# Attention with negated, pre-scaled scores, the sink as a 129th score column, and one copy of the whole product with the values

## Chip, core and metric

One Trainium2 chip, one NeuronCore. The metric is device time in microseconds (us), the median of several runs. The engines are PE (matrix products; PEld is its weight load), DVE (vector), ACT (scalar functions), POOL and SP (which issues the DMAs here). They run side by side and wait for each other by semaphores. Each one works through its own queue in order.

## The reference, cut to what matters

The program is one step of a two-layer decoder on 512 prompt rows and 8 sample rows. Layer 0 is a recurrent mixer, which the change leaves alone. Layer 1 is attention in a sliding window of 128 keys with 32 query heads in 4 groups of 8, and a learned "sink" score per head, which takes part in the softmax and has no value row:

```
ATTN_SCALE = HEAD_DIM ** -0.5        # 64 ** -0.5
def sink_softmax(s, sinks):
    sink = ...                        # one score per head, broadcast to every query
    pr = jax.nn.softmax(jnp.concatenate([s, sink], axis=-1), axis=-1)
    return pr[..., :-1]
def one_block(args):                  # 128 queries against 128 or 256 keys
    mask = in_band & ((cidx >= WINDOW) | (n > 0))
    s = jnp.einsum('bqhgd,bkhd->bhgqk', qn, kn) * ATTN_SCALE
    s = jnp.where(mask, s, -jnp.inf)
    pr = sink_softmax(s, sinks)
    return jnp.einsum('bhgqk,bkhd->bqhgd', pr, vn)
```

Each layer ends in `mix @ w_out`, a norm, and a gated embedding. The activations stand transposed in the kernel: features on partitions, rows (520 = 512 + 8) along the free axis.

## The kernel before

**Products in three parts.** An fp32 product is made of three faster ones: weights and activations are split into a high and a low half. ACT casts the high half (`wh` of the weights `wr`), DVE or POOL subtracts it for the low half (`wl`), and PE adds `wh` x high, `wl` x high and `wh` x low in a PSUM pair `pj`. These projection matmuls (128x260) are most of PE's work. Their operands `xs` are the split activations of the layer's input, `og` the split outputs of the attention, which the products with `w_out_b` read.

**The attention.** Layer 1 runs eight units `u` of four query heads. A unit has four projection tiles (two of queries, two of gates `z`). `query` applies the rotation to a tile `tmp` and splits each head's 64 rows into high and low, stacked on 128 partitions of a tile `g`. Then `block(u, st, n, osb)` runs for each of the four blocks `n` of 128 queries. It makes the scores of four heads in two PSUM banks `ph` (`xr` holds the keys); ACT copies them into the score tile `W` [128, 4, 128], and DVE's copy_predicated takes the masked part: the previous block's keys, or `neg` in the first block. DVE then finds the maximum `nm` (tile `an`), joins it with the sink (`sinkb`), forms the sink's exponent `es` (tile `ae`) and negates the maximum. ACT takes four exponentials with the scale 1/8, whose sums go to `den` (tile `ad`), and one of the sink. DVE adds that, takes the reciprocal and multiplies `W`. PE transposes `W` (`ident` on the left), the result is split into high and low (two tiles `g`), masked copies of these are made with `tmask`, and PE multiplies them with the values `V`. The two halves of the 128 result rows (high and low value columns) are added: ACT copies a half of the rows to `both` (tile `m`), and DVE adds the other half, into `osb` (tile `ao`). After the fourth block, `osb` is gated and split into the unit's `og`.

`W` lies in the buffers of the tags b2 (3) and b3 (2), which other stages share. `sample_b` serves the 8 sample rows of four units at a time, in one short sequence of its own (`qs`, `bm`, `bd`, `tmp`, `bo`).

**What sets the order.** The code does not issue instructions directly. `Plan.enter` records each with its reads and writes, and `Plan.issue` then sets the order of every engine's queue by a list schedule with costs written into the program. It places an instruction where it would start earliest by these costs. An instruction that may run on DVE or POOL (`nc.either`) is put on one of them there. All of PE's matmuls, projections and attention alike, stand in one queue in that order, so that a matmul that is not ready holds all behind it. Because every instruction is issued at line 162, the profile names that line throughout, and the groups are told apart by their tiles.

Of the kernel before, what the change touches and what calls it, by code (L numbers as in the profile page):

```python
# [18 lines left out]
P = 128  # L19
D_MODEL = 1024  # L20
KC = D_MODEL // P
SEQ = 512
# [6 lines left out]
HD = 64  # L29
EPS = 1e-6  # L30
SCALE = HD ** -0.5
NEG = -1.0e30
SWAP = list(range(8, 16)) + list(range(0, 8)) + list(range(16, 32))

PRE0, PRE1, POST0, POST1, KVG, ONORM, LB0, LB1 = 0, 8, 16, 24, 32, 40, 56, 72
# [322 lines left out]
class Step:  # L358
# [53 lines left out]
    def more_consts(self):  # L412
        nc, cp, i = self.nc, self.cp, self.i
        self.ident = cp.tile([P, P], F32, name="ident")
        nc.sync.dma_start(self.ident, i["ident"])
        self.pairmask = cp.tile([P, 64], F32, name="pairmask")
        nc.sync.dma_start(self.pairmask, i["pairmask"])
        self.ones_r = cp.tile([P, P], F32R, name="ones_r")
        nc.scalar.copy(self.ones_r, self.ones.to_broadcast([P, P]))
        self.lmask = self.plan.tile(self.sp, [P, 6, 64], I32, "lmask", "m", 1)  # L420
        nc.sync.dma_start(self.lmask.rearrange("p a b -> p (a b)"), i["lmask"])
        self.neg = cp.tile([P, 1], F32, name="neg")
        nc.vector.memset(self.neg, NEG)
        self.pmask = cp.tile([P, P], I32, name="pmask")
        nc.sync.dma_start(self.pmask, i["pmask"])
        self.tmask = cp.tile([P, 2, P], F32, name="tmask")
        nc.sync.dma_start(self.tmask.rearrange("p a b -> p (a b)"), i["tmask"])
        self.sinkb = cp.tile([P, 32], F32, name="sinkb")
        nc.sync.dma_start(self.sinkb, i["sinkb"])
        self.sinks = cp.tile([P, KVH // 2], F32, name="sinks")  # L430
        nc.sync.dma_start(self.sinks, i["sinks"])

# [131 lines left out]

    def rsqrt_small(self, ps, rows, cols, n, tag):
        nc = self.nc
        ms = self.small(tag + "m", [P, 8])
        nc.vector.tensor_scalar(ms[:rows, :cols], ps, 1.0 / n, EPS, op0=ALU.mult, op1=ALU.add)
        r = self.small(tag + "r", [P, 8])
        nc.gpsimd.tensor_tensor(r[:rows, :cols], ms[:rows, :cols], self.mhalf[:rows, :cols], op=ALU.pow)  # L570
        return r

# [518 lines left out]
    def unit_proj(self, u, xs, st, done):  # L1091

        nc = self.nc
        kvh = u // 2
        rows = slice((kvh % 2) * HD, (kvh % 2 + 1) * HD)
        st["Q"], st["z"], st["og"] = [], [], []

        def query(c):
            def evac(ps):
                q = self.tmp_()  # L1100
                self.rope(ps, self.C, self.S, q)
                for a in range(2):
                    s = self.g_(F32R)
                    me = slice(a * HD, (a + 1) * HD)
                    other = slice((1 - a) * HD, (2 - a) * HD)
                    nc.scalar.copy(s[me, :SEQ], q[me, :SEQ])
                    nc.vector.tensor_tensor(
                        s[other, :SEQ], q[me, :SEQ], s[me, :SEQ].bitcast(F32), op=ALU.subtract
                    )
# [43 lines left out]
    def block(self, u, st, n, osb):  # L1153


        nc = self.nc
        kvh = u // 2
        keys = P if n == 0 else 2 * P
        k0 = 0 if n == 0 else (n - 1) * P
        W = self.small("b3", [P, 4, P], 2) if n % 3 else self.small("b2", [P, 4, P], 3)  # L1160
        for a in range(2):
            ps = self.bank().rearrange("p (a k) -> p a k", a=2)
            for b in range(2):
                q = st["Q"][2 * a + b][:, n * P : (n + 1) * P]
                for K, s0, s1 in ((self.Kh, True, False), (self.Kl, False, True)):
                    nc.tensor.matmul(ps[:, b, :keys], q, K[kvh][:, k0 : k0 + keys], start=s0, stop=s1)
            w = W[:, 2 * a : 2 * a + 2]
            if n == 0:
                nc.scalar.copy(w, ps[:, :, :P])
                nc.vector.copy_predicated(  # L1170
                    w,
                    self.pmask.unsqueeze(1).to_broadcast([P, 2, P]),
                    self.neg.unsqueeze(1).to_broadcast([P, 2, P]),
                )
            else:
                nc.scalar.copy(w, ps[:, :, P:])
                nc.vector.copy_predicated(w, self.pmask.unsqueeze(1).to_broadcast([P, 2, P]), ps[:, :, :P])
        nm = self.small("an", [P, 4])
        nc.vector.tensor_reduce(nm, W, AX.X, ALU.max)
        sk = self.sinkb[:, 4 * u : 4 * u + 4]  # L1180
        nc.vector.scalar_tensor_tensor(nm, nm, SCALE, sk, op0=ALU.mult, op1=ALU.max)
        es = self.small("ae", [P, 4])
        nc.vector.tensor_tensor(es, sk, nm, op=ALU.subtract)
        nc.vector.tensor_scalar(nm, nm, -1.0, None, op0=ALU.mult)
        den = self.small("ad", [P, 4])
        for j in range(4):
            nc.scalar.activation(
                W[:, j], W[:, j], AF.Exp, bias=nm[:, j : j + 1], scale=SCALE, accum_out=den[:, j : j + 1]
            )
        nc.scalar.activation(es, es, AF.Exp)  # L1190
        nc.vector.tensor_tensor(den, den, es, op=ALU.add)
        nc.vector.reciprocal(den, den)
        nc.either.tensor_tensor(W, W, den.unsqueeze(2).to_broadcast([P, 4, P]), op=ALU.mult)
        pt = self.bank()
        for pos, j in enumerate((0, 2, 1, 3)):
            nc.tensor.transpose(pt[:, pos * P : (pos + 1) * P], W[:, j], self.ident)
        hi, lo = (self.g_(F32R, SEQ) for x in range(2))
# [3 lines left out]
        if n:  # L1201
            for x in (hi, lo):
# [5 lines left out]
                    op=ALU.mult,  # L1208
                )
                parts.append((2 * n - 1 if n < 3 else 4, y))  # L1210
        po = self.bank()
        for x, (vn, pp) in enumerate(parts):
            V = self.V[vn][:, kvh]
            nc.tensor.matmul(po, V, pp, start=x == 0, stop=x == len(parts) - 1)
        both = self.small("m", [P, 512], 1)
        for a in range(2):
            me = slice(a * HD, (a + 1) * HD)
            other = slice((1 - a) * HD, (2 - a) * HD)
            t = both[:, a * 256 : (a + 1) * 256]
            nc.scalar.copy(t[me], po[other, a * 256 : (a + 1) * 256])  # L1220
            nc.vector.tensor_tensor(
                osb[me, :, n * P : (n + 1) * P],
                po[me, a * 256 : (a + 1) * 256].rearrange("p (c t) -> p c t", c=2),
                t[me].rearrange("p (c t) -> p c t", c=2),
                op=ALU.add,
            )
        if n < NCH - 1:
            return
        for c, (hi, lo) in enumerate(self.og_b(u, st)):
            w = osb[:, c]  # L1230
# [396 lines left out]
```

## Time and profile before

| what | value |
|---|---|
| median of 3 runs | 1131.54 us (1131.02 to 1131.56) |
| profiled execution, its own time | 1133.34 us |
| its span, first to last instruction | 1131.5 us |
| PE / DVE / ACT / POOL busy | 1106.6 / 966.1 / 749.7 / 121.8 us |
| mean granted TensorE clock | 0.995 |
| DMA | 137.56 MB, mean 122 GB/s |

The span runs from the first layer (to about 600 us) over its gates and the keys and values to the attention units with their output products (about 660 to 1060) and the last gates. A row of a group of instructions reads: engine, operation, out<-in, shapes, count, then busy us and mean ns of one, then the engine's idle time before them and what ended it. A row of waits reads: engine and tile that waited, what released it, total us, number of waits, the longest. A row of stretches reads: from:to, length, then busy us and (xcount) of PE, PEld, DVE, ACT and POOL, then the granted clock, the DMA share and GB/s. A row of the timeline reads: start, duration, engine, operation, and in brackets the idle time before it and its releaser.

### The profile page before, as it was taken

To read this page: it belongs to the slowest core of one execution; us is meant where nothing else is said; L and a number is where in the kernel's file an instruction comes from. 1 tells how busy PE (TensorE), PEld (TensorE's weight loads), DVE (VectorE), ACT (ScalarE), POOL (GpSimd) and SP (SyncE) were. 2 spreads that over 40 slices of the span, in tenths; PEclk is the share of its full clock that TensorE was granted. 3 is DMA by queue.
4 is the path that set the end of the run, shared out by engine and by line. 5 is a ranking of instruction groups with operands and counts; after the bars stand their busy time and mean duration, and the time that the engine had idled before them with its cause. 6 is when DMAs were issued, how large, how long until landed. Compare 5 with 4: busy or idle time off the path is not lost.

```text
span 1131.5 us, 23984 instructions
## 1 busy us (share of the span) xinstructions
PE 1106.6 (98%) x8999; PEld 1088.3 (96%) x8999; DVE 966.1 (85%) x2218; ACT 749.7 (66%) x1990; POOL 121.8 (11%) x188
## 2 busy tenths in 40 slices
PE   8999999999999999999999999999989999999998
PEld 7999999999999999999999999999989999999997
DVE  6998888758888588888879989999988998998983
ACT  7878777657775477777736657767666764764551
POOL 0121121112211122111100000110100000000000
PEclk9999999999999999999999999999989999999999
DMA  8433524334432343434445442212212222312532
GB/s 292 150 135 115 187 99 170 110 136 152 139 126 97 118 165 134 143 125 138 141 151 204 127 152 91 77 57 86 84 39 75 76 75 75 107 49 73 205 104 86
DMA packets 53821, 137.56 MB, mean 122 GB/s; under 512 B 10948, under 2 KB 18124, under 8 KB 53704
## 3 DMA queue, kind: packets, MB, share of 16 engines
q1 hardware_dynamic: 53704, 136.02, 35.7%
q8 instruction: 71, 1.16, 0.4%
q14 instruction: 46, 0.38, 0.1%
HBM read 119.22 MB, written 16.77 MB: 120 GB/s over the span
## 4 chain that ended last, share of the span: by engine, by line
PE 70%; DVE 20%; ACT 5%; issue 3%; DMA 1%; POOLq 0%; SPq 0%; POOL 0%; DVEq 0%; ACTq 0%
PE pj L162 56%; PE ph L162 14%; DVE g L162 4%; DVE tmp L162 3%; DVE wl L162 3%; DVE b L162 2%; ACT b L162 1%; DVE ao L162 1%; DVE an L162 1%; DVE xr L162 1%; DMA wr<-in_w_pg 1%; DVE x L162 1%; ACT tmp L162 1%; ACT g L162 1%; ACT wh L162 1%
## 5 line engine op out<-in xcount | busy, mean ns | idle before, releaser
L162 PE MATMUL pj<-xs,wh 128*128 128x260 f32 x3328 | 571.2, 285 | 0.8 <-DVE x L162 0.3
L162 PEld LDWEIGHTS pj<-xs,wh 128*128 128x128 f32 x3328 | 468.9, 189 | 4.1 <-ACT xs L162 1.2
L162 PE MATMUL pj<-xs,wl 128*128 128x260 f32 x1664 | 346.6, 285 | 0.0
L162 PEld LDWEIGHTS pj<-xs,wl 128*128 128x128 f32 x1664 | 260.7, 189 | 0.8
L162 ACT CAST wh<-wr 128x512 fp32r<-128x512 f32 x288 | 176.3, 618 | 97.9 <-PE pj L162 87.0
L162 DVE TENSOR_TENSOR wl<-wr,wh 128x512 fp32r<-128x512 f32 x273 | 188.1, 692 | 31.3 <-ACT wh L162 29.9
L162 PE MATMUL pj<-og,wh 128*128 128x260 f32 x1056 | 187.3, 287 | 2.5 <-ACT g L162 1.4
L162 PEld LDWEIGHTS pj<-og,wh 128*128 128x128 f32 x1056 | 152.9, 190 | 4.7 <-DVE x L162 1.8
L162 PE MATMUL pj<-og,wl 128*128 128x260 f32 x512 | 108.0, 286 | 0.0
L162 ACT ACTIVATE tmp<-pj 128x520 f32<-128x520 f32 (+1 forms) x93 | 48.0, 528 | 55.0 <-PE pj L162 54.5
L162 PEld LDWEIGHTS pj<-og,wl 128*128 128x128 f32 x512 | 81.3, 190 | 0.6
L162 ACT ACTIVATE sb<-sb,nv 128x128 f32<-128x128 f32 x128 | 68.4, 564 | 0.2
L162 ACT ACTIVATE sb<-sb,g 128x128 f32<-128x128 f32 x128 | 64.3, 561 | 4.5 <-DVE sb L162 4.2
L162 DVE COPY_PREDICATED xr<-lmask,ph 128x128 f32<-128x128 int32 x192 | 55.2, 323 | 5.3 <-PE ph L162 4.1
L162 PE MATMUL pj<-xs,b 128*128 128x260 f32 x384 | 52.2, 285 | 2.8 <-ACT b L162 2.0
L162 DVE TENSOR_TENSOR x<-x,pj 128x520 f32<-128x520 f32 (+1 forms) x80 | 46.0, 582 | 10.6 <-PE pj L162 9.9
L162 ACT ACTIVATE b<-b,an 128x128 f32<-128x128 f32 x128 | 50.4, 396 | 2.9 <-DVE an L162 2.7
L162 PEld LDWEIGHTS pj<-xs,b 128*128 128x128 f32 x384 | 48.2, 188 | 3.9 <-ACT b L162 2.4
L162 PE MATMUL ph<-g,b 128*128 128x512 f32 x112 | 46.1, 424 | 3.5 <-DVE g L162 2.6
L162 PE MATMUL ph<-b,xr 128*128 128x256 f32 (+1 forms) x288 | 47.5, 281 | 0.0
L162 DVE TENSOR_TENSOR xr<-xr,b 128x256 f32<-128x256 f32 x96 | 41.2, 430 | 4.8 <-PE ph L162 3.0
L162 ACT COPY xr<-ph 32x64 f32<-32x64 f32 (+2 forms) x128 | 39.7, 313 | 8.5 <-PE ph L162 6.1
(208 smaller groups left out, 1861.6 us busy)
## 6 DMA issues: line engine op xcount, KB each, us to landing
wr<-in_w_in_a SPq DMA_DIRECT2D x64, 512.0 KB, 3.6
sb<-sd SPq DMA_DIRECT2D x32, 512.0 KB, 4.7
wr<-in_w_in_b SPq DMA_DIRECT2D x32, 512.0 KB, 3.5
sb<-in_state SPq DMA_DIRECT2D x16, 512.0 KB, 5.0
out_st_s<-sb SPq DMA_DIRECT2D x16, 512.0 KB, 2.9
wr<-in_w_out_a SPq DMA_DIRECT2D x16, 512.0 KB, 3.8
wr<-in_w_pg SPq DMA_DIRECT2D x16, 512.0 KB, 4.3
wr<-in_w_out_b SPq DMA_DIRECT2D x16, 512.0 KB, 3.5
```

The costliest lines, as they stand in the source:

```text
L162: op = Op(len(self.ops), self.level, on, [lambda c=c: c(*a, **k) for c in calls], [self.price(e, name, ins, a, k) for e in on], on[0] == " ...
```

## The change

- The query split writes -1/8 times the queries, so the scores leave PE negated and scaled. The masked value becomes +1e30 (`far`), the maximum a minimum, and the exponentials take scale -1 with the minimum as bias.
- `W` gets a 129th column per head, filled by ACT with the negated sink ahead of the scores. Minimum and sums of the exponentials cover it, so that the join, the sink's exponent, its exponential, its addition and the negation of the maximum go away. `sinkb` is negated once at the start.
- ACT copies all 128 rows of the product with the values at once; DVE's two additions take one half from PSUM and the other from that copy.
- Two small tiles of the sample rows' norm in layer 0 (tag "nn") have one buffer in place of two.

```
# query
-  nc.scalar.copy(s[me, :SEQ], q[me, :SEQ])
-  nc.vector.tensor_tensor(s[other, :SEQ], q[me, :SEQ], s[me, :SEQ].bitcast(F32), op=ALU.subtract)
+  nc.scalar.activation(s[me, :SEQ], q[me, :SEQ], AF.Copy, scale=-SCALE)
+  nc.vector.scalar_tensor_tensor(
+      s[other, :SEQ], q[me, :SEQ], -SCALE, s[me, :SEQ].bitcast(F32), op0=ALU.mult, op1=ALU.subtract)
# block
-  W = self.small("b3", [P, 4, P], 2) if n % 3 else self.small("b2", [P, 4, P], 3)
+  W = self.small("b3", [P, 4, P + 1], 2) if n % 3 else self.small("b2", [P, 4, P + 1], 3)
+  nc.scalar.copy(W[:, :, P], self.sinkb[:, 4 * u : 4 * u + 4])
...
-  nc.vector.tensor_reduce(nm, W, AX.X, ALU.max)
-  sk = self.sinkb[:, 4 * u : 4 * u + 4]
-  nc.vector.scalar_tensor_tensor(nm, nm, SCALE, sk, op0=ALU.mult, op1=ALU.max)
-  es = self.small("ae", [P, 4])
-  nc.vector.tensor_tensor(es, sk, nm, op=ALU.subtract)
-  nc.vector.tensor_scalar(nm, nm, -1.0, None, op0=ALU.mult)
+  nc.vector.tensor_reduce(nm, W, AX.X, ALU.min)
   den = self.small("ad", [P, 4])
   for j in range(4):
       nc.scalar.activation(
-          W[:, j], W[:, j], AF.Exp, bias=nm[:, j : j + 1], scale=SCALE, accum_out=den[:, j : j + 1])
-  nc.scalar.activation(es, es, AF.Exp)
-  nc.vector.tensor_tensor(den, den, es, op=ALU.add)
+          W[:, j], W[:, j], AF.Exp, bias=nm[:, j : j + 1], scale=-1.0, accum_out=den[:, j : j + 1])
   nc.vector.reciprocal(den, den)
...
   both = self.small("m", [P, 512], 1)
+  nc.scalar.copy(both, po)
   for a in range(2):
-      t = both[:, a * 256 : (a + 1) * 256]
-      nc.scalar.copy(t[me], po[other, a * 256 : (a + 1) * 256])
-      nc.vector.tensor_tensor(osb[me, :, n * P : (n + 1) * P], po[me, ...], t[me], op=ALU.add)
+      nc.vector.tensor_tensor(osb[me, :, n * P : (n + 1) * P], of(po, other), of(both, me), op=ALU.add)
# more_consts
+  nc.vector.tensor_scalar(self.sinkb, self.sinkb, -1.0, None, op0=ALU.mult)
```

Since the costs are recorded from the code, the planner sets another order for the whole attention stage; the first layer's order stays. In the rows below, the numbers behind a tile's name are its own; before and after count differently.

First place, on PE, where unit 3's projections end and the products with `w_out_b` of units 0 and 1 run. Before: behind the scores of unit 3's last block (`ph_2051`) come the transposes of unit 2's last block (`b2_1957`), then its products with the values (`ph_1968`), with the sample rows' product (`ph_2005`) between.

```order
L162 MATMUL ph_2051_2147<-xr_1678_1774,g_1992_2088 128x256
L162 MATMUL ph_2051_2147<-xr_1682_1778,g_1992_2088 128x256
L162 MATMUL ph_2051_2147<-xr_1678_1774,g_1993_2089 128x256
L162 MATMUL ph_2051_2147<-xr_1682_1778,g_1993_2089 128x256
L162 MATMUL ph_1963_2059<-ident_109,b2_1957_2053 128x128 x4
L162 MATMUL ph_1968_2064<-g_1964_2060,b4_1652_1748 128x512
L162 MATMUL ph_2005_2101<-tmp_2004_2100,b3_1995_2091 128x16 x8
L162 MATMUL ph_1968_2064<-g_1965_2061,b4_1652_1748 128x512
L162 MATMUL ph_1968_2064<-g_1966_2062,b2_1653_1749 128x512
L162 MATMUL ph_1968_2064<-g_1967_2063,b2_1653_1749 128x512
L162 MATMUL pj_2091_2187<-og_1786_1882,wh_2017_2113 128x260
```

After, at the same place (the end of the projection `pj_2004`, the sample rows' product `ph_1993`): the transposes are those of unit 3's first block (`b2_2013`), and 19 projection matmuls follow before its product with the values, five rows of which are shown.

```order
L162 MATMUL ph_2037_2133<-xr_1682_1778,g_1981_2077 128x256
L162 MATMUL pj_2004_2100<-xs_1621_1717,wh_1996_2092 128x260 x2
L162 MATMUL ph_1993_2089<-tmp_1992_2088,b3_1983_2079 128x16 x8
L162 MATMUL ph_2018_2114<-ident_109,b2_2013_2109 128x128 x4
L162 MATMUL pj_2071_2167<-og_1782_1878,wh_1999_2095 128x260
L162 MATMUL pj_2071_2167<-og_1782_1878,wl_2000_2096 128x260
L162 MATMUL pj_2071_2167<-og_1783_1879,wh_1999_2095 128x260
L162 MATMUL pj_2071_2167<-og_1784_1880,wh_1999_2095 128x260
L162 MATMUL pj_2071_2167<-og_1784_1880,wl_2000_2096 128x260
```

Unit 2's last block (`b2_1946` after) has its transposes 51 rows further up now, inside that projection:

```order
L162 MATMUL pj_2004_2100<-xs_1606_1702,wl_1977_2073 128x260 x2
L162 MATMUL pj_2004_2100<-xs_1607_1703,wh_1976_2072 128x260
L162 MATMUL ph_1984_2080<-qs_1697_1793,b4_1982_2078 128x16 x8
L162 MATMUL ph_1951_2047<-ident_109,b2_1946_2042 128x128 x4
L162 MATMUL pj_2004_2100<-xs_1607_1703,wh_1976_2072 128x260
```

The block has moved from the end of the projections into them.

Second place, on DVE, the same block (unit 2, `n` = 3), from its reduction on. Before: up to the negated maximum, for which ACT's exponentials wait.

```order
L162 TENSOR_REDUCE an_1960_2056<-b2_1957_2053 128x4
L162 TENSOR_SCALAR tmp_2001_2097<-tmp_2001_2097,bd_2002_2098 128x128
L162 SCALAR_TENSOR_TENSOR an_1960_2056<-an_1960_2056,sinkb_116 128x4
L162 TENSOR_TENSOR g_1952_2048<-ph_1950_2046,g_1951_2047 128x512
L162 TENSOR_TENSOR g_1953_2049<-g_1951_2047,tmask_115 128x512
L162 TENSOR_TENSOR g_1954_2050<-g_1952_2048,tmask_115 128x512
L162 TENSOR_TENSOR ae_1961_2057<-sinkb_116,an_1960_2056 128x4
L162 COPY_PREDICATED b2_2025_2121<-pmask_114,neg_113 128x256
L162 TENSOR_SCALAR an_1960_2056<-an_1960_2056 128x4
```

After: from the reduction, for which the exponentials wait, to the reciprocal of the sums.

```order
L162 TENSOR_REDUCE an_1949_2045<-b2_1946_2042 128x4
L162 SCALAR_TENSOR_TENSOR g_1970_2066<-tmp_1968_2064,g_1970_2066 64x512
L162 SCALAR_TENSOR_TENSOR g_1971_2067<-tmp_1968_2064,g_1971_2067 64x512
L162 TENSOR_TENSOR tmp_1978_2074<-pj_1972_2068,ropeC_1630 128x520
L162 STREAM_SHUFFLE tmp_1979_2075<-pj_1972_2068 128x520
L162 TENSOR_TENSOR g_1941_2037<-ph_1939_2035,g_1940_2036 128x512
L162 TENSOR_TENSOR tmp_1979_2075<-tmp_1979_2075,ropeS_1631 128x520
L162 TENSOR_TENSOR wl_1997_2093<-wr_1975_2071,wh_1996_2092 128x512
L162 TENSOR_TENSOR tmp_1978_2074<-tmp_1978_2074,tmp_1979_2075 128x520
L162 TENSOR_TENSOR g_1943_2039<-g_1941_2037,tmask_115 128x512
L162 RECIPROCAL ad_1950_2046<-ad_1950_2046 128x4
```

The three small instructions between the reduction and the exponentials are gone, and so is the addition ahead of the reciprocal.

Third place, on ACT: after, the sink's column of a score tile (`b2_2047`) stands behind the cast (`CAST g_1952`) of the transposes of the tile that had the buffer before (`b2_1946`).

```order
L162 CAST g_1952_2048<-ph_1951_2047 128x512
L162 COPY b2_2047_2143<-sinkb_116 128x4
L162 COPY b2_2013_2109<-ph_2015_2111 128x2x128
L162 COPY b3_2023_2119<-ph_2025_2121 128x2x128
L162 ACTIVATE be_1988_2084<-be_1988_2084 128x1
```

Before, ACT's first instruction on a score tile was the copy of its first scores; now it is the sink's column.

More of the change, by code (lines that the diff above doesn't have):

```diff
@@ L31 @@
 SCALE = HD ** -0.5
-NEG = -1.0e30
+FAR = 1.0e30
 SWAP = list(range(8, 16)) + list(range(0, 8)) + list(range(16, 32))
@@ L421, in more_consts @@
         nc.sync.dma_start(self.lmask.rearrange("p a b -> p (a b)"), i["lmask"])
-        self.neg = cp.tile([P, 1], F32, name="neg")
-        nc.vector.memset(self.neg, NEG)
+        self.far = cp.tile([P, 1], F32, name="far")
+        nc.vector.memset(self.far, FAR)
         self.pmask = cp.tile([P, P], I32, name="pmask")
@@ L566, in rsqrt_small @@
         nc = self.nc
-        ms = self.small(tag + "m", [P, 8])
+        bufs = 1 if tag == "nn" else 2
+        ms = self.small(tag + "m", [P, 8], bufs)
         nc.vector.tensor_scalar(ms[:rows, :cols], ps, 1.0 / n, EPS, op0=ALU.mult, op1=ALU.add)
-        r = self.small(tag + "r", [P, 8])
+        r = self.small(tag + "r", [P, 8], bufs)
         nc.gpsimd.tensor_tensor(r[:rows, :cols], ms[:rows, :cols], self.mhalf[:rows, :cols], op=ALU.pow)
@@ L1105, in evac @@
                     other = slice((1 - a) * HD, (2 - a) * HD)
-                    nc.scalar.copy(s[me, :SEQ], q[me, :SEQ])
-                    nc.vector.tensor_tensor(
-                        s[other, :SEQ], q[me, :SEQ], s[me, :SEQ].bitcast(F32), op=ALU.subtract
+                    nc.scalar.activation(s[me, :SEQ], q[me, :SEQ], AF.Copy, scale=-SCALE)
+                    nc.vector.scalar_tensor_tensor(
+                        s[other, :SEQ], q[me, :SEQ], -SCALE, s[me, :SEQ].bitcast(F32), op0=ALU.mult, op1=ALU.subtract
                     )
@@ L1166, in block @@
                     nc.tensor.matmul(ps[:, b, :keys], q, K[kvh][:, k0 : k0 + keys], start=s0, stop=s1)
-            w = W[:, 2 * a : 2 * a + 2]
+            w = W[:, 2 * a : 2 * a + 2, :P]
             if n == 0:
@@ L1172, in block @@
                     self.pmask.unsqueeze(1).to_broadcast([P, 2, P]),
-                    self.neg.unsqueeze(1).to_broadcast([P, 2, P]),
+                    self.far.unsqueeze(1).to_broadcast([P, 2, P]),
                 )
@@ L1187, in block @@
             nc.scalar.activation(
-                W[:, j], W[:, j], AF.Exp, bias=nm[:, j : j + 1], scale=SCALE, accum_out=den[:, j : j + 1]
+                W[:, j], W[:, j], AF.Exp, bias=nm[:, j : j + 1], scale=-1.0, accum_out=den[:, j : j + 1]
             )
-        nc.scalar.activation(es, es, AF.Exp)
-        nc.vector.tensor_tensor(den, den, es, op=ALU.add)
         nc.vector.reciprocal(den, den)
+        W = W[:, :, :P]
         nc.either.tensor_tensor(W, W, den.unsqueeze(2).to_broadcast([P, 4, P]), op=ALU.mult)
@@ L1218, in block @@
             other = slice((1 - a) * HD, (2 - a) * HD)
-            t = both[:, a * 256 : (a + 1) * 256]
-            nc.scalar.copy(t[me], po[other, a * 256 : (a + 1) * 256])
[L1221 to L1226, printed above, removed]
+            of = lambda x, rows: x[rows, a * 256 : (a + 1) * 256].rearrange("p (c t) -> p c t", c=2)
+            nc.vector.tensor_tensor(osb[me, :, n * P : (n + 1) * P], of(po, other), of(both, me), op=ALU.add)
         if n < NCH - 1:
```

## The prediction

> **What bounds the kernel now.** I read the page's first part, then busy time by stage, then what TensorE waits for in the stage that the change touches.
>
> ```profile
> PE 1106.6 (98%) x8999; PEld 1088.3 (96%) x8999; DVE 966.1 (85%) x2218; ACT 749.7 (66%) x1990; POOL 121.8 (11%) x188
> 660.00:1060.00 400.00, 391.69 (x3095) 380.50 (x3094) 371.44 (x863) 257.98 (x781) 20.46 (x16) 0.99 0.26 85
> ```
>
> The second row is the attention stage: PE (391.69 of 400) and DVE (371.44) are both nearly full, ACT is not. A busy PE may be slow, so the pace matters:
>
> ```profile
> 948.38 14.11 PE pj L162 x118
> ```
>
> In this piece of the chain 118 projection matmuls follow each other at 14.11 / 118 = 0.120 us: PE alone sets that pace. The change removes no matmul (PE's order has 8654 instructions before and after), so it can only win time in which PE waits or runs slowly. PE's waits in the stage:
>
> ```profile
> PE ph L162 <- DVE ae L162: 3.4, 2, 2.9
> PE ph L162 <- DVE g L162: 2.6, 4, 0.9
> PE ph L162 <- ACT g L162: 0.7, 1, 0.7
> PE ph L162 <- DVE b L162: 0.6, 1, 0.6
> ```
>
> Together 7.3 us, every one behind DVE or ACT; one wait of 2.9 is more than a third. The timeline there, and the clock around it in stretches of 10.24 us:
>
> ```profile
> 822.42 1.13 PE L162 MATMUL ph<-xr,g 128*128 128x256 f32 x8
> 826.43 0.88 PE L162 MATMUL ph<-ident,b 128*128 128x128 f32 x4 [2.88 <-DVE ae L162]
> 827.99 0.79 PE L162 MATMUL ph<-g,b 128*128 128x512 f32 x1 [0.67 <-ACT g L162]
> ...
> 816.44:826.68 10.24, 6.92 (x53) 6.60 (x54) 9.98 (x32) 7.88 (x32) 0.00 (x0) 1.00 0.16 52
> 826.68:836.92 10.24, 9.57 (x40) 8.44 (x39) 7.02 (x20) 5.26 (x24) 0.00 (x0) 0.50 0.01 2
> 836.92:847.16 10.24, 10.24 (x82) 9.93 (x82) 8.80 (x22) 7.75 (x20) 0.00 (x0) 1.00 0.16 54
> ```
>
> PE waits 2.88 us for the transposes of unit 2's last block, 0.67 for the next product, and right behind the long wait the granted clock is 0.50 for 10.24 us. PE was busy for 9.57 of these, so about 9.57 x 0.5 = 4.8 us went to the clock. The event costs 2.88 + 0.67 + 4.8 = 8.3 us, twice the other waits of the stage (7.3 - 3.55 = 3.7).
>
> Why the transposes were late, on DVE (ACT's first exponential among the rows):
>
> ```profile
> 817.80 0.69 DVE L162 TENSOR_REDUCE an<-b 128x4 f32<-128x512 f32 x1
> 818.59 0.16 DVE L162 SCALAR_TENSOR_TENSOR an<-an,sinkb 128x4 f32<-128x4 f32 x1
> 820.47 0.16 DVE L162 TENSOR_TENSOR ae<-sinkb,an 128x4 f32<-128x4 f32 x1
> 820.93 0.16 DVE L162 TENSOR_SCALAR an<-an 128x4 f32<-128x4 f32 x1
> 822.23 0.40 ACT L162 ACTIVATE b<-b,an 128x128 f32<-128x128 f32 x1
> 824.72 0.16 DVE L162 TENSOR_TENSOR ad<-ad,ae 128x4 f32<-128x4 f32 x1
> 825.40 0.17 DVE L162 RECIPROCAL ad<-ad 128x4 f32<-128x4 f32 x1
> 825.60 0.69 DVE L162 TENSOR_TENSOR b<-b,ad 128x512 f32<-128x512 f32 x1
> ```
>
> The maximum was there at 818.49. Three operations of 0.16 us each followed, with other work between them in DVE's queue, and the exponentials could not start before 821.09. The reciprocal then stood behind the addition of the sink's term and a reduction.
>
> **The change, part by part.** Prices:
>
> ```profile
> L162 DVE SCALAR_TENSOR_TENSOR an<-an,sinkb 128x4 f32<-128x4 f32 x32 | 6.0, 189 | 0.2
> L162 DVE TENSOR_TENSOR ae<-sinkb,an 128x4 f32<-128x4 f32 x32 | 5.9, 187 | 0.2
> L162 DVE TENSOR_SCALAR an<-an 128x4 f32<-128x4 f32 x32 | 5.3, 164 | 0.5
> L162 DVE TENSOR_TENSOR ad<-ad,ae 128x4 f32<-128x4 f32 x32 | 4.9, 156 | 2.5 <-ACT b L162 2.1
> L162 ACT ACTIVATE ae<-ae 128x4 f32<-128x4 f32 x32 | 6.2, 198 | 8.1 <-DVE ae L162 7.9
> L162 ACT COPY zb<-g 128x8 f32<-128x8 f32 x16 | 3.1, 195 | 4.2 <-DVE g L162 3.9
> L162 ACT COPY m<-ph 64x256 f32<-64x256 f32 x64 | 23.5, 367 | 13.2 <-PE ph L162 10.6 <-DVE ao L162 1.7
> L162 ACT CAST g<-ph 128x512 fp32r<-128x512 f32 x32 | 18.6, 582 | 9.8 <-PE ph L162 9.5
> L162 DVE SCALAR_TENSOR_TENSOR ao<-ao,g 128x512 f32<-128x512 f32 x16 | 10.5, 686 | 0.1
> L162 DVE TENSOR_TENSOR og<-ao,og 128x512 fp32r<-128x512 f32 x14 | 9.3, 684 | 0.2 <-ACT og L162 0.2
> L162 DVE SCALAR_TENSOR_TENSOR tmp<-x,vec,R 128x260 f32<-128x260 f32 x32 | 14.6, 482 | 0.0
> L162 DVE TENSOR_TENSOR tmp<-tmp,g 128x260 f32<-128x260 f32 x32 | 12.8, 425 | 16.9 <-ACT tmp L162 16.7
> L162 DVE COPY_PREDICATED b<-pmask,ph 128x256 f32<-128x256 int32 x48 | 20.5, 442 | 1.8 <-ACT b L162 1.5
> L162 ACT ACTIVATE b<-b,an 128x128 f32<-128x128 f32 x128 | 50.4, 396 | 2.9 <-DVE an L162 2.7
> L162 ACT ACTIVATE sb<-sb,nv 128x128 f32<-128x128 f32 x128 | 68.4, 564 | 0.2
> ```
>
> DVE loses four small operations in each of 32 blocks: 6.0 + 5.9 + 5.3 + 4.9 = 22.1 us. The planner gives three wl subtractions back from POOL and moves two masks there (counts from the order), about 0.7 us more for DVE. Net some 21 us of its 371, all beside PE except where PE waits.
>
> ACT loses 32 exponentials of the sink (6.2) and gains 32 copies of it; the nearest row is the 128x8 copy, 195 ns, so 6.2: nothing. Each copy takes a score tile as soon as it is free, so it might hold up ACT's queue. But in the new order it stands behind ACT's own cast of the transposes that free the tile, and waits for nothing more; the four first stand behind the first layer.
>
> The whole product: two copies of 367 ns become one; the nearest row, 128x512 from PSUM, has 582, so 0.15 us less ACT work a block, 4.9 in all, off the path. The first addition waits 0.21 us longer, the second 0.15 less; both lie at the block's end.
>
> The scaled split of the queries: scalar_tensor_tensor for tensor_tensor. At 128x512 with a constant the rows are 686 and 684, at 128x260 with a scalar pointer 482 and 425. Bounds 0 and 32 x 0.06 = 1.9 us of DVE; I take 0, the form with a constant is this one. ACT's scaled copy for a cast: 0, with the 32 x 0.15 saved above as its cover.
>
> Rows of 129: 4 more elements in a reduction of 512, nothing. The pitch shows in no row. Nearest pair: ACT at a stride of 8 elements takes 564 ns for 128 against 396, 1.4 times; here the elements stay adjacent, so I take 0 and keep 1.4 for a rival.
>
> The negation of sinkb adds one small DVE operation early (0.16 us) behind a load:
>
> ```profile
> L162 SPq DMA_DIRECT2D sinkb<-in_sinkb x1: 349/349/349, 15.9 to 15.9; - x1
> DMA to landing us min/median/max: 5.0/5.0/5.0
> 19.14 3.94 DVE L162 TENSOR_TENSOR acc<-acc,tmp 128x520 f32<-128x520 f32 x5
> ```
>
> It lands at 20.9; the five sums ahead of it on DVE end at 23.1. No wait.
>
> What becomes time: the event. In the new order unit 2's last block has its transposes among the projections of unit 3, long ahead of the place; what stands at the place are unit 3's first transposes, followed by 19 projection matmuls (2.3 us) where before the next product followed at once. So the 0.67 goes, and the clock's 4.8 with it unless another long wait comes. What is late next is that first block of unit 3: behind its exponentials ACT must wait for unit 2's last product. From that product to these transposes stand 27 projection matmuls of 0.12 and 17 smaller of at most 1.13 / 8 = 0.14, some 5 us; the rows that must end between them are ACT's copy and a cast (0.58 each), then on DVE a weight subtraction and two tensor operations of 128x512 (0.69 each), an addition (0.42), a reciprocal (0.17) and the product (0.69): 4.5 us, 5 with the second addition. I expect a wait of up to 1.5 there, 1 in the sum: 8.3 - 1 = 7.3. Of the other 3.7 us, behind a DVE that is 5% lighter, I take 1.0, and give 0.8 back for waits of the new order. Sum: 7.3 + 1.0 - 0.8 = 7.5 us. The profiled execution took 1133.34 (span 1131.5), so 1125.8 for it; the median of the runs is 1.8 lower: 1131.54 - 7.5 = 1124.0.
>
> The Trainium skill, "TensorE: Matmul & The Clock Gate", Part 1, says the clock halves after an idle window of about 3.4 us, and that the windows run free. This trace agrees in the length (10.24 us are three of 3.413) but its wait was 2.88, so the phase must have helped. By that rule alone the drop could vanish while the wait stayed, which would give 4.8 of the 8.3.
>
> **The rivals.**
> (1) The event moves: unit 3's first transposes are 2.9 us late or more, and the clock falls again. For it: 12 projections stand behind them in PE's queue, and cover and need are nearly equal. Against: it needs 2.9 beyond the cover, and DVE has fewer rows there. Time: 1131.5 - 0.2 - (0 to 2) = about 1130.5.
> (2) PE's other waits fall too, all 3.7: 1131.5 - 8.3 - 3.7 = 1119.5. Against: 2.6 of it waits for the halves of the transposes, which the change does not touch.
> (3) The pitch of 129 slows each pass over the scores. At 1.4, two masked copies of 0.44, reduction 0.68 and product 0.69 cost 0.9 us a block more, 29 on DVE against 22 saved; DVE then has 378 of 400 us and PE waits more often: with the event back and half as many waits again, 1131.5 + 4 = 1135.5. It decides from 1.3 times on.
> (4) A second clock drop in the reshuffled order, beside the first: 1131.5 + 8 = 1139.5.
>
> **How the numbers follow.** The forecast with its spread (1120 to 1128.5) 0.72, (2) 0.05, (1) 0.13, (3) 0.06, (4) 0.04. About 0.2% (2.3 us) is what a measurement of this kernel can tell from no change. Faster: 0.72 + 0.05 + a quarter of (1) = 0.80; same the rest of (1), 0.10; slower 0.06 + 0.04 = 0.10. The range 1119 to 1131 leaves out (3), (4) and the ends.
>
> **What would show it.** The four small groups gone from DVE, its busy time in the stage some 20 us lower; no granted clock under 0.9 between 660 and 1060; no PE wait over 1.5 us. Rows of 129 at the old durations. If PE's 10.24 us at 0.50 stand at another place, (1) or (4) was right; if the score rows are longer, (3).

## The result, and the profile after

The changed kernel takes 1117.99 us (1117.45 to 1118.27) against 1131.55 (1131.02 to 1131.84) for the kernel before: a ratio of 0.988, with a 95% interval of 0.9863 to 0.9897. That is 13.6 us less. The forecast was 7.5 us less, and its range ended at 1119. Two runs of later experiments, disturbed to two and three times the time of the others, are left out of their medians.

The profiled executions differ by more, spans of 1131.5 and 1116.2. Before's profiled execution was 1.8 us above the median of its runs. Matched matmul by matmul with other traces, 1.0 us of that is a wait at 652 and 0.7 a wait at 1109. Both are waits for a weight whose load came late (ACT's cast of it waited 1.4 and 5.5 us for the DMA), and other traces of the same code wait less there.

The page's first part and the attention stage, in the same columns as before's rows, then the two stretches of 10.24 us:

```profile
PE 1100.5 (99%) x8999; PEld 1085.8 (97%) x8999; DVE 951.4 (85%) x2092; ACT 740.9 (66%) x1958; POOL 121.7 (11%) x187
660.00:1060.00 400.00, 396.76 (x3201) 388.82 (x3200) 369.57 (x773) 257.97 (x766) 20.86 (x17) 1.00 0.27 88
816.44:826.68 10.24, 9.99 (x83) 9.70 (x83) 9.63 (x27) 9.93 (x42) 0.00 (x0) 1.00 0.17 53
826.68:836.92 10.24, 10.24 (x85) 10.07 (x84) 9.15 (x26) 8.84 (x31) 0.00 (x0) 1.00 0.18 53
```

In the same 400 us PE now runs 3201 matmuls instead of 3095, and the granted clock stays at 1.00. The two stretches that held the long wait and the slow clock now hold 83 and 85 matmuls, where 53 and 40 stood.

The place itself on PE's timeline, and the longest of PE's waits from 640 us on:

```profile
820.08 1.85 PE L162 MATMUL ph<-tmp,b 128*128 128x16 f32 x16
821.78 0.64 PE L162 MATMUL ph<-ident,b 128*128 128x128 f32 x4
824.95 0.73 PE L162 MATMUL ph<-g,b 128*128 128x512 f32 x2 [0.25 <-ACT bo L162]
...
PE ph L162 <- POOL rsr L162: 0.9, 1, 0.9
PE pj L162 <- DVE x L162: 0.9, 2, 0.5
PE ph L162 <- DVE g L162: 0.9, 1, 0.9
PE ph L162 <- ACT b L162: 0.5, 1, 0.5
```

Unit 3's first transposes (821.78) come just in time, with no wait in brackets. The waits behind `ae` (3.4) are gone, and those behind `g` fell from 2.6 in four waits to 0.9 in one. The new forms, by group:

```profile
L162 ACT ACTIVATE b<-b,an 128x129 f32<-128x129 f32 x128 | 50.6, 398 | 3.4 <-DVE an L162 3.3
L162 ACT COPY m<-ph 128x512 f32<-128x512 f32 x32 | 18.7, 585 | 15.1 <-PE ph L162 11.5 <-DVE ao L162 1.9 <-issue 1.5
L162 ACT COPY b<-sinkb 128x4 f32<-128x4 f32 x32 | 5.7, 196 | 0.0
L162 DVE TENSOR_REDUCE an<-b 128x4 f32<-128x516 f32 x32 | 21.7, 678 | 0.4
```

The exponentials take 398 ns (396 before), the reduction 678 (679), the whole copy 585 (the bound used was 582), the sink's copy 196 (195).

To place the gain I set the start of each matmul in the two traces side by side by its number in PE's queue. After is ahead by 0.8 us at the stage's first units, by 2.1 at matmul 6600 (before's 812.6), by 11.4 at matmul 6800 (847.1), and by 14.6 at the stage's end. So 9.3 fall at the event, 1.3 ahead of it and 3.2 behind it: 13.8, close to the gain of the runs.

### The profile page after: what moved, and what is told of

Its sections match the earlier page's. It is cut to its first block, busy times and chain, and to the rows that moved or that the text cites. A ratio compares the mean times of both kernels' runs of the same rounds, so it can differ in the third digit from the quotient of the medians.

```text
span 1116.2 us, 23808 instructions
## 1 busy us (share of the span) xinstructions
PE 1100.5 (99%) x8999; PEld 1085.8 (97%) x8999; DVE 951.4 (85%) x2092; ACT 740.9 (66%) x1958; POOL 121.7 (11%) x187
## 4 chain that ended last, share of the span: by engine, by line
PE 84%; DVE 10%; ACT 3%; issue 2%; DMA 1%; POOLq 0%; SPq 0%; POOL 0%; ACTq 0%; DVEq 0%
PE pj L162 67%; PE ph L162 17%; DVE wl L162 1%; DVE g L162 1%; DVE tmp L162 1%; DVE xr L162 1%; DVE b L162 1%; DVE x L162 1%; DMA wr<-in_w_pg 1%; ACT g L162 1%; ACT tmp L162 1%; DMA wr<-in_w_in_b 0%; DVE xs L162 0%; ACT og L162 0%; DMA x<-in_xT 0%
## 5 line engine op out<-in xcount | busy, mean ns | idle before, releaser
L162 DVE TENSOR_TENSOR wl<-wr,wh 128x512 fp32r<-128x512 f32 x276 | 190.4, 693 | 36.7 <-ACT wh L162 35.2
L162 ACT ACTIVATE b<-b,an 128x129 f32<-128x129 f32 x128 | 50.6, 398 | 3.4 <-DVE an L162 3.3
L162 DVE TENSOR_TENSOR g<-g,b 128x256 f32<-128x256 f32 x96 | 42.3, 441 | 3.4 <-POOL b L162 1.5
```

The source lines that it names most:

```text
L162: op = Op(len(self.ops), self.level, on, [lambda c=c: c(*a, **k) for c in calls], [self.price(e, name, ins, a, k) for e in on], on[0] == " ...
```

## Experiments

The planner sets a new order for every change of the code, so most kernels here hold one order fixed and change only the work in it. `pre` and `post` are instructions put ahead of or behind a planned one; `skip` leaves out the planned one.

**1. The new softmax in the old order.** Before's order on every engine; the half copies stay.

```
# before, planned as before; then
+ for op in (join, es_sub, negate, es_exp, den_add): op.skip = True
+ first_score_copy.pre = [ACT copy of -sink into W[:, :, 128]]
  query split, minimum, exponentials: as in the change
```

> Every engine keeps the order of before word for word; the sink is a column of the scores, and the four small DVE operations and the sink's exponential of each block are left out of the queues where they stood. The two half copies of the product stay. Theory W (work: a lighter DVE queue and a shorter way from the reduction to the transposes win the time, in whatever order): the long wait at 826 falls from 2.9 us under 1.5, the granted clock stays up, 1120 to 1123 us. Theory O (order: the planner's new order wins the time): the transposes of unit 2's last block still stand right behind the scores, a wait over 2 us and the clock's drop stay, 1128 to 1131 us.

1127.89 us, ratio 0.9966 (0.9953 to 0.9978), some 4 us less, just under theory O's range. PE's wait at the place, and the stretch of slow clock behind it:

```profile
823.13 0.63 PE L164 MATMUL ph<-ident,b 128*128 128x128 f32 x4 [2.85 <-ACT b L164]
824.09:834.33 10.24, 9.90 (x40) 9.18 (x41) 5.99 (x17) 5.54 (x27) 0.00 (x0) 0.50 0.00 0
```

The wait is as long as it was (2.88), only its releaser has changed from DVE's sink operations to ACT's exponentials. A shorter chain in the old order doesn't remove the event.

**2. The old small operations in the new order.** Four small DVE operations a block are put back, which the order was not planned for; the results they compute are not needed.

```
# after, planned as after; then
+ reduction.post = [3 DVE operations, 128x4]
+ reciprocal.pre = [1 DVE operation, 128x4]
```

> Every engine keeps the order of after word for word; three small DVE operations on the minimum are put right behind each reduction, and one on the sums right ahead of each reciprocal, in place and without effect on the values, so that DVE has the 22 us of before again and the way is some 0.5 us longer a block. Theory W: a third to two thirds of the gain is lost, 1122 to 1127 us. Theory O: 1118 to 1120 us.

1141.59 us (1140.78 to 1142.4), ratio 1.0088 (1.0072 to 1.0103): slower than before, and 23.6 above after, for four groups that took 22.1 us in before's rows.

```profile
660.00:1060.00 400.00, 381.43 (x3013) 367.60 (x3012) 372.01 (x852) 247.56 (x740) 20.20 (x15) 1.00 0.24 79
...
PE ph L163 <- DVE b L163: 5.6, 10, 1.8
PE ph L163 <- DVE g L163: 4.7, 6, 1.4
PE ph L163 <- ACT wh L163: 2.7, 2, 1.4
PE pj L163 <- DVE x L163: 1.8, 2, 1.3
```

PE runs 188 matmuls fewer in the 400 us than after does. No wait is over 1.8 and the clock stays at 1.00. The loss is many short waits for DVE. The new order needs the lighter DVE. Both theories missed the size: neither range reaches 1130. And the load put back is more than the old one: DVE is busy 974.1 us here, 8.0 more than in before (966.1), probably because the operations now stand right behind one another. So 23.6 is more than the old operations in their old places would cost.

**3. The whole copy alone, and 4. the sink column alone,** each planned anew from its own work.

```
# 3: before, with after's lines from nc.scalar.copy(both, po) on
# 4: after, with before's two half copies
```

> Before with the one copy of the whole product alone, planned anew. Theory W: ACT is not the limit, so what is seen is the luck of another order, 1127 to 1133 us. Theory C (the copy's shorter ACT work wins a good part): 1120 to 1125 us.

> After with the two half copies of before, planned anew: the scaled queries and the sink's column alone. Theory W: 1117 to 1121 us. Theory C: 1124 to 1129 us. Theory O: anything between 1117 and 1131, since the order is another one again.

1124.94 us (0.9944, 0.9929 to 0.9958) and 1120.92 us (0.9907, 0.9892 to 0.9921). The sink column alone meets theories W and O. The copy alone lies under theory W's range, and at the edge of theory C's, but not for theory C's reason: 0.15 us a block, on an engine that is idle a third of the time, "won" 6.6 us with a new order, while in a fixed order the copy is worth about 1.5 (experiment 5). The stage in both, and a short stretch of slow clock of the copy alone with the 3.41 us ahead of it:

```profile
660.00:1060.00 400.00, 394.02 (x3135) 383.71 (x3135) 375.70 (x879) 253.27 (x756) 17.88 (x15) 1.00 0.26 86
660.00:1060.00 400.00, 396.10 (x3170) 385.95 (x3170) 365.05 (x758) 262.50 (x792) 25.81 (x20) 1.00 0.27 88
...
808.05:811.46 3.41, 3.17 (x27) 2.92 (x26) 2.85 (x9) 2.50 (x8) 0.20 (x1) 1.00 0.47 154
811.46:814.88 3.42, 3.42 (x18) 3.42 (x18) 3.26 (x6) 3.35 (x12) 0.00 (x0) 0.50 0.38 104
```

Matched by matmul, the copy alone loses 2.4 us from the stage's start to matmul 6600, gains 7.1 from there to 6800, and some 0.8 more by the stage's end. Its plan happens not to hold the long wait. It has a slow stretch of its own, but only of 3.41 us.

**5. All the new work in the old order.**

```
# experiment 1, and
+ half_copy_0.skip = half_copy_1.skip = True
+ half_copy_0.pre = [ACT copy of all of po]
  the two additions, in their places: as in the change
```

> Before's order on every engine, word for word, with all of after's work in it: the softmax as in the first experiment, and the whole copy of the product with the values in place of the two half copies (the second one's place is left empty). Theory O (what the order was planned for decides; work taken away inside an order moves PE only where a wait shortens): the transposes of unit 2's last block still stand behind ACT's exponentials, the wait stays at 2.5 to 3, the clock still falls, and the time is that of the first experiment less 0 to 2: 1126 to 1128. Theory A (ACT's queue is what was left of the wait once DVE's small operations were gone): 32 x 0.15 us less of ACT work brings the exponentials forward, the wait falls under 2 us, the clock stays up and the time falls to 1119 to 1121, with little left for the order.

1126.37 us, ratio 0.9937 (0.9916 to 0.9958): 5.2 below the 1131.55 of the first comparison, 6.0 below the before of its own. After, with the same work in its own order, is another 8.4 lower. The waits:

```profile
PE ph L164 <- ACT b L164: 2.3, 1, 2.3
PE ph L164 <- DVE g L164: 1.4, 3, 0.5
...
823.04:833.28 10.24, 9.57 (x40) 8.44 (x38) 6.44 (x17) 4.98 (x24) 0.00 (x0) 0.50 0.01 2
```

The event is still there, 0.6 shorter. The waits for the halves of the transposes (`g`) fell from 2.6 to 1.4, though no instruction of theirs changed or moved: DVE gets to them sooner. From matmul 6600 to 6800 this kernel gains 1.4 us where after gains 9.3, so 7.9 of the 8.4 us by which the orders differ are the event. In the rest of the stage it gains 2.5 us ahead of the event and 1.8 behind it, 4.3 together, nearly after's 4.5, and all of it in before's order. Theory O holds, with a wait a little under its 2.5.

**6. and 7. Unit 3's first transposes made late,** by two or five passes of DVE over the score tile (values unchanged).

```
# after, planned as after; unit 3, n = 0:
+ reciprocal.pre = [DVE tensor_tensor(W, W, W, max)] * 2      # or * 5
```

> After, word for word, with two passes of DVE over the score tile (0.65 us each) put ahead of the reciprocal of unit 3's first block, whose transposes came just in time. It makes one PE wait of about 1.3 us at the place of before's long one. Theory E (the event's price is the wait plus a clock drop that needs a wait near 3 us): 1.3 us and no drop, 1118.0 + 1.3 = 1119.3. Theory S (DVE stands so full behind this point that its lateness is passed on to several waits): more than 2.5 us, 1120.5 or above.

> The same with five passes (3.3 us). Theory E: a PE wait of about 3.3 us at this place, the granted clock at 0.5 for 3.4 or 10.24 us behind it, 3.3 + (1.7 to 5.1): 1123 to 1126.4. If the clock stays up with such a wait: 1121.3, and the clock's 4.8 us of the prediction's first term were not tied to the wait's length alone. Theory S: 1127 or above.

1119.14 us (1118.73 to 1120.2) and 1123.00 us (1121.71 to 1124.27). PE's timeline with two passes, then with five, and the slow stretch of the latter:

```profile
823.73 0.66 PE L163 MATMUL ph<-ident,b 128*128 128x128 f32 x4 [0.62 <-DVE b L163]
827.46 0.73 PE L163 MATMUL ph<-g,b 128*128 128x512 f32 x2 [0.79 <-ACT bo L163]
```

```profile
824.62 1.12 PE L163 MATMUL ph<-ident,b 128*128 128x128 f32 x4 [2.81 <-DVE b L163]
823.62:830.45 6.83, 5.83 (x25) 5.70 (x26) 6.03 (x18) 3.50 (x17) 0.00 (x0) 0.50 0.23 77
```

Two passes cost 1.3 us at the place (matched by matmul), no more than they last. Five cost 5.1 there: 2.8 of wait and 2.3 of clock, which is 0.39 for each of the 5.83 us in which PE was busy at half clock. Nothing of either is passed on to later waits: theory E holds for both. The second is rival (1) brought about by hand.

**8. One small operation a block put back,** 32 in all.

```
# after, planned as after
+ reciprocal.pre = [1 DVE operation, 128x4]
```

> After, word for word, with one small operation of DVE (128x4, 0.16 us) put back ahead of each block's reciprocal, which the order was not planned for; 32 of them, 5.1 us of DVE. Theory O (after's order fits the DVE work it was planned for so closely that what is added there shows almost in full, as the second experiment's 22 us gave 23.6): about 5 us, 1122 to 1124. Theory F (there is some slack to be used up first, and only a large overload shows): under 2 us, 1118 to 1120.

1121.63 us, ratio 0.990 (0.9873 to 0.9927), 3.6 above after for a DVE that was busy 956.2 us instead of 951.4. The time lies between the two theories. Matched by matmul it loses up to 0.5 at a time all through the stage, 4.1 in all. Among its waits from 640 us on:

```profile
PE ph L163 <- DVE b L163: 1.2, 4, 0.6
PE ph L163 <- DVE g L163: 1.0, 1, 1.0
```

In after's order, then, there is hardly any slack: most of what DVE is given beyond the plan shows in the time.

**9 to 12, 16 and 17. Other plans of the same work.** One constant of the planner (how long a matmul's operands must have been there to put it first) is changed, on before and on after.

```
-HAND = 0.3
+HAND = 0.28        # or 0.20, 0.40
```

> Before with all its work, planned again with one constant of the planner moved from 0.30 to 0.28 us: the time by which the operands of a matmul must have been ready to be put ahead of others. This reorders about as many of PE's rows as the change did. Theory L (the long wait with its clock drop is an accident of the one order that before has; a new plan of the same work loses it as well): no wait over 2 us near 820, no drop there, and the time falls by 5 to 9 to 1123 to 1127; then most of the change's gain is not owed to its lighter work. Theory P (the planner could only fit the blocks before the place because the work became lighter): the wait stays over 2 us at this place or another like it, and the time within 2 us of before.

> The same with the constant at 0.20. Theory L: 1122 to 1129, without a wait of over 2 us between 800 and 850. Theory P: 1130 to 1134, with one.

> The same with the constant at 0.40, which reorders the most. Theory L: 1122 to 1130, with long waits at other places or none. Theory P: 1130 to 1136, with a long wait near 820 and a lower clock behind it.

> After with all its work, planned again with the constant at 0.20. Theory L (one order's accident is some microseconds either way, and what the work itself is worth is the difference between the two kernels over several plans): 1116 to 1126, by accident; the difference to before with the same constant is the work's own, about 5. Theory P: within 2 us of after, 1116 to 1120, and 12 or more below before at the same constant.

> After with all its work, planned again with the planner's constant at 0.28, the value that made before's plan the slowest of four (1136.5). Theory M (the plan is worth some 10 us either way for the old work; the new work is less at its mercy, because DVE is not late so often): 1117 to 1123. Theory N (any plan can go wrong as far as before's did): 1123 to 1130, with clock drops in the attention stage.

> The same at 0.40, where before took 1133.9. Theory M: 1117 to 1123, with no clock drop in the attention stage. Theory N: 1123 to 1130.

| constant | before | after | difference |
|---|---|---|---|
| 0.30 | 1131.5 | 1118.0 | 13.6 |
| 0.28 | 1136.5 (1.0035, 1.0022 to 1.0048) | 1119.6 (0.9892, 0.9876 to 0.9909) | 16.9 |
| 0.20 | 1124.5 (0.9933, 0.9918 to 0.9948) | 1116.8 (0.9863, 0.9848 to 0.9878) | 7.7 |
| 0.40 | 1133.9 (1.0019, 1.0008 to 1.0031) | 1122.9 (0.9918, 0.9900 to 0.9936) | 11.0 |

Ratios are to before at 0.30. The last cell is the median of three runs. The plan alone is worth 12 us for the old work and 6 for the new. Neither L nor P holds as I wrote it; theory M was met by both plans that it was written for (after at 0.28 and 0.40). No other plan of the old work has a wait over 1.2 us in or behind the attention stage, so the long wait belongs to one plan of four; but of the three without it only the plan at 0.20 is faster (1124.5, as theory L has it). All four plans of the new work are faster than all four of the old, by 12.3 us in the mean, more than the 5 that the work gains in a fixed order. Three of the four old plans have a half-clock stretch near the event's place (10.24 us at 0.30, two of 6.83 at 0.28, 3.41 at 0.40); none of the four new plans has one in the stage.

At 0.28 before's plan shows something else. Here is PE's timeline and two stretches:

```profile
814.44 1.82 PE L162 MATMUL ph<-qs,b 128*128 128x16 f32 x14 [0.84 <-ACT qs L162]
812.53:815.94 3.41, 2.57 (x23) 2.35 (x22) 3.26 (x8) 3.07 (x8) 0.00 (x0) 1.00 0.45 154
815.94:822.77 6.83, 6.83 (x34) 6.83 (x34) 5.87 (x23) 3.88 (x19) 0.21 (x1) 0.50 0.21 77
```

The clock falls behind a wait of 0.84 us. Ahead of this wait PE ends its matmuls of 128 columns and runs seven projections; what stands behind it are matmuls of 16 columns, which count as busy.

**13 to 15. The wait filled.** Matmuls of 512 columns, whose results the transposes overwrite, are put ahead of the late transposes.

```
# before, planned as before; unit 2, n = 3 (13, 14)
# after with five passes (7), unit 3, n = 0 (15)
+ first_transpose.pre = [PE matmul(pt, ones_r, Kh[3])] * 10     # 14: * 3
```

> Before, word for word, with ten matmuls of 512 columns (constant operands, 0.236 us each at the full clock, 2.4 in all) put into PE's queue ahead of the late transposes of unit 2's last block. They write the bank that the transposes then overwrite, and their results are used nowhere. DVE is as late as before, so PE's next useful matmul starts when it did. Theory C (the clock falls when PE streams less than about 0.38 of a window of 3.41 us; a long wait is only one way to that): the window's share rises from 0.07 to about 0.75, no drop, and the time falls by what the drop cost, 4 to 5 us, to 1127 to 1128. Theory W (the late data are what costs; the clock is a small part): within 2 us of before, 1130 to 1132.

> The same with three such matmuls (0.7 us), which leave 2.2 us of the wait. Theory C: the share of the window rises to about 0.28, still under the bound, and the drop stays: 1130.5 to 1132, with some runs lower where the free-running windows cut the wait in two. Theory I (any matmul that breaks the idle stretch keeps the clock up): no drop, 1127 to 1128, like ten.

> After with the five passes ahead of the reciprocal of unit 3's first block, as in the late experiment, and the ten filling matmuls ahead of these late transposes. Theory C: the wait is filled, no drop; 1118.0 + 2.9 = 1120.9, some 2 below the late experiment's 1123.0. Theory W: the same 1123.

Ten: 1129.32 us, ratio to before 0.998 (0.997 to 0.999), 2.4 us less. Three: 1130.32 us, 0.9989 (0.998 to 0.9998). Ten in the late kernel: 1121.44 us (1120.89 to 1122.22), and no drop; matched by matmul the place costs 3.5 us instead of the late kernel's 5.1. (The two kernels' ratios, 0.9911 and 0.9906, don't show these 1.6: before scattered from 1130.57 to 1136.21 in the late kernel's comparison.) Before with ten, three windows and PE's timeline:

```profile
823.34:826.75 3.41, 2.22 (x12) 1.39 (x10) 3.19 (x14) 3.29 (x16) 0.00 (x0) 1.00 0.41 150
826.75:830.16 3.41, 3.12 (x21) 2.68 (x22) 3.34 (x8) 1.86 (x10) 0.00 (x0) 1.00 0.00 0
830.16:833.57 3.41, 3.41 (x18) 3.41 (x17) 2.40 (x11) 2.47 (x12) 0.00 (x0) 0.50 0.01 2
...
822.39 2.46 PE L1206 MATMUL ph<-xr,ones_r 128*128 128x512 f32 x10
825.36 0.66 PE L163 MATMUL ph<-ident,b 128*128 128x128 f32 x4 [0.51 <-DVE b L163]
826.69 0.50 PE L163 MATMUL ph<-g,b 128*128 128x512 f32 x1 [0.68 <-ACT g L163]
827.48 1.96 PE L163 MATMUL ph<-tmp,b 128*128 128x16 f32 x16 [0.29 <-DVE g L163]
829.28 0.94 PE L163 MATMUL ph<-g,b 128*128 128x512 f32 x3
```

With three the drop stays, 6.83 us long, against theory I. The window ahead of it and the drop:

```profile
824.20:827.61 3.41, 1.15 (x5) 0.61 (x5) 3.26 (x11) 3.41 (x18) 0.00 (x0) 1.00 0.30 119
827.61:834.44 6.83, 6.72 (x28) 6.43 (x29) 4.24 (x14) 3.38 (x17) 0.00 (x0) 0.50 0.00 1
```

Ten matmuls shorten the slow stretch from 10.24 us to 3.41 and win 2.5 us at the place, matched by matmul; the data come as late as before. Theory C expected it to vanish and 4 to 5 us to be won. The first window was filled as planned; the drop that was left came behind the next one, with 3.12 us of busy PE. That window streams 4 x 512 + 16 x 16 = 2304 columns; at the pace of the projections (260 columns in 0.120 us) these need 1.06 us, 0.31 of the window.

**18. After once more.**

> After as it is, on the same chip as the two others: 1117.5 to 1118.5 by both theories. It sets the scale for them.

1117.57 us (1117.3 to 1118.31), ratio 0.9877 (0.9862 to 0.9892). This is as expected. The new work's plan at 0.20 (1116.83, 1115.92 to 1117.03) is the lowest measured. The interval of its ratio (0.9848 to 0.9878) overlaps that of after's, so that it beats before is shown, that it beats after is not.

## Why the prediction was wrong, step by step

- **What bounds the kernel** held: PE ran all its matmuls in less time, and only waits, some of them too short to be listed, and slow clock went.
- **The event, 8.3 less 1 for a new wait: 9.3 was won.** The mechanism was right: the block moved ahead of the place, the clock stayed up. Its sizes were off. The wait of up to 1.5 at unit 3's first transposes is no wait at all, and 0.25 at the product behind. And the place held two waits more that I left out of this term: 0.71 by the gap between matmuls, at 816 (the list's 0.6 behind `b`), and some 0.3 ahead of the sample rows' product, which is no row of before (experiment 13 lists it with 0.29). The clock's part was too high: at half clock two projections take 0.43 us, 0.215 each, so 9.57 busy us lose 1 - 0.120 / 0.215 = 0.44 each, 4.2 and not 4.8. By the late kernel's 0.39 it is 3.7. With these sizes the event comes to 2.88 + 0.67 + 4.2 + 0.71 + 0.3 - 0.25 = 8.5; what else is in the 9.3 stays open.
- **"Of the other 3.7 us of waits I take 1.0, and give 0.8 back": this step failed.** 0.2 was forecast; in the stage outside the event 4.5 was won (1.3 ahead, 3.2 behind). My argument against rival (2) was that 2.6 of it waits for the halves of the transposes, "which the change does not touch". It touches the queue they stand in. Experiment 5 shows this with no row moved: 2.6 became 1.4, and 4.3 us were won outside the event. The lighter queues were worth those 4.3 where the step had 1.0; 4.0 of it is there already in experiment 1, matched the same way, which leaves ACT's half copies as they were. On balance nothing was given back: the planner fits an order to the lighter queue, and experiments 2 and 8 show how closely. Rival (2), at a chance of 0.05, came nearest, but had no term beyond the listed waits (and the 3.7 left out the list's fifth row, 0.4 behind DVE's `x`). Part of the 4.5 lies in waits too short to be rows: PE's busy time fell by 6.1 us (1106.6 to 1100.5), 1.9 more than the clock's 4.2. Which of them, no row tells.
- **DVE's "some 20 us" less: 14.7 by the page** (966.1 to 951.4), and 10.5 in experiment 5. The durations of the four groups sum to 22.1 as forecast, but in before's trace other operations of DVE run during half of that: only 10.8 us of its busy time are covered by these four groups alone. Put back where they stand right behind one another (experiment 2) they made DVE 22.7 busier, and the time 23.6 longer.
- **The edits costed at nothing** were that: the 129th column, the scaled split, the sink's copies. The copy in a fixed order was worth some 1.5 us (1127.89 to 1126.37, from two comparisons whose runs overlap), perhaps not quite nothing.
- **Rivals (3) and (4)** didn't come. Rival (1) did not come either, but would have cost 5 us and not 8 (experiment 7). The 12 projections that it puts behind the transposes are 19 in the order, as the sum has them.
- **"By that rule alone the drop could vanish while the wait stayed":** filling the wait did two thirds of that, for 2.4 us. The free-running window of the Trainium skill, "TensorE: Matmul & The Clock Gate", Part 1, fits all traces here: every drop that ended within a trace lasted 3.41, 6.83 or 10.24 us. The "idle window" that the prediction took from there doesn't fit: PE was busy for up to 3.17 of the 3.41 us ahead of a drop (experiment 3).

What the gain consists of, then: some 5 us are the lighter work with no row moved (experiment 5). The other 8 came with the new order, and most of them are one event that the old plan had. That the event went is partly an accident of planning (three other plans of the old work don't have the long wait, the best of them reaches 1124.5, and a change as small as the whole copy loses it too); that four plans of the new work all lie below the four of the old isn't. How much of the 8 a given replanning would have won can't be told from four plans.

## What to carry to other kernels

Where a planner sets the order, measure a change twice: in the old order, with the work alone changed, and over several plans of both kernels; one pair of plans mixes what the work is worth with the luck of a plan (here 12 us). A queue that is 93% full is a resource that all its users share: when it gets lighter, look also at the waits for operations that the change doesn't name. Work added behind the planner's back cost most of its length here (3.6 of 5.1 us, and 23.6 for 22), while work taken out behind its back gained a fraction (5 to 6 us for 22).

## What was not expected of the hardware

By these traces the clock follows how much PE streams in a window, not the longest wait. I cut all 20 traces (40 to 1095 us) into windows of 3.413 us in step with the clock's own changes, and took for each the columns that PE streamed, at 0.4615 ns a column (260 in 0.120 us), over the window's length. Of 6183 windows 22 were followed by a half-clock window, and all 22 had shares of 0.368 or less. Of the 6161 others two lay below that (0.310 in before planned at 0.20, 0.361 in after planned at 0.40), and the next had 0.386; so the bound is near 0.37, and not without exceptions. A wait of 2.9 us halves the clock, and so does a wait of 0.84 beside 14 matmuls of 16 columns; waits of 0.6 and 0.8 in two neighbouring windows (experiment 6) don't. The clock returned after the first half-clock window above the bound. (Columns are counted there with the same 0.4615 ns, though at 0.215 us a projection a full window has no more than about 0.56: 0.401 to 0.561 where the window ended the drop, 0.366 at most where the drop went on.) Experiments 13 to 15 are tests of this by intervention, with a bound of about 0.38 written down before they ran, and all three agree with it; elsewhere it is a reading of the traces.
